# A hybrid diffusion backbone on one core: gate matrices without their zero halves, their products on quarters of the array

## The chip, the cores and the metric

The kernel runs on one core of one Trainium2 chip. The metric is the device time of one execution in microseconds (us). TensorE (PE) multiplies matrices into PSUM, which has eight banks here; VectorE (DVE), ScalarE (ACT) and GpSimd (POOL) compute; SyncE (SP) issues every DMA.

## The reference

Two layers work on 256 latent tokens with 256 context tokens ahead of them, 1024 channels, all in fp32. Each layer projects its modulated, normalised input to three mixers, merges them and ends with a mixture of experts. The change touches the first mixer, a gated linear recurrence that runs forwards and backwards (the direction index is di):

```python
def lru_scan(u, wa, ba, wx, bx, lam, h0, reverse):
    ub = u.reshape(B, L, LRU_HEADS, LRU_BW)             # 16 heads of 64 channels
    r = sigmoid(einsum('blhi,hij->blhj', ub, wa) + ba)
    i = sigmoid(einsum('blhi,hij->blhj', ub, wx) + bx)
    log_a = -LRU_C * r * softplus(-lam)
    a = exp(log_a)
    b = sqrt(-expm1(2.0 * log_a)) * (i * u)
    a_cum, b_cum = associative_scan(_linear_combine, (a, b), reverse=reverse, axis=1)
    return a_cum * h0[:, None, :] + b_cum
```

Every head multiplies its 64 channels by a 64x64 matrix, once for the r gate (wa) and once for the i gate (wx), for each direction.

## The kernel before

Activations lie transposed: 128 channels on the partitions, 512 tokens (context, then latent) along the free axis. `Dense` (from L152) runs the large projections. A step loads a block of 1024x256 weights (`raw`, two buffers), splits it on ACT (`whi`, L179 or L225) and DVE (`wlo`, L180 or L226) into a high and a low part, and multiplies: 48 matmuls of 512 columns into a pair of PSUM tiles `pT` (`Dense.T`, L207 to L209; `Dense.first`, L238 to L240, is the first two steps of layer 0 at once, half of the contraction at a time), or 96 of 256 columns into `pN` (`Dense.N`, L258 to L260). The weights of a step are split while the step before runs. After every 12 matmuls of a T step and 24 of an N step `tick` (L458) runs one piece of pending work from a list; the mixers' element work and their small products get between the large ones in this way. In layer 0 ticks also run a piece of `mod_vec`, the later modulation vectors (`psmod`, L412, fp32 products on column groups of 32).

`lru` (L588) makes the recurrence in four blocks of 256 channels. `lru_block` (L596) takes the projections `ax` and `ay` of its block, convolves `ax` to `u` (two tiles of 128 channels, kk = 0 and 1, two heads each), and leaves seven pieces of work for later ticks: four calls of `gates(kk, di)`, one square root, two scans. `gates` (L615) multiplies `u` by the r and the i matrix (`zr` L622, `zi` L623), each a PSUM tile of 512 columns, and hands on to ACT: `tr` (L625) from zr, `lT` (L627), `lQ` (L628), then `ti` (L631) from zi. A bank is free again when ACT has read it. The two heads of a tile are multiplied at once: `load_lru_w` (L575) lays their 64x64 matrices on the diagonal of a 128x128 one; POOL zeroes the tile (L578), and eight DMAs fill the diagonal (L584). One tile holds one block's matrices, and each block loads the next one's.

All PSUM tiles come from one pool of eight banks. At the start `norm1` (L517) transposes the normalised input into eight PSUM tiles `psu` (L539), which are all the banks; ACT and DVE copy them out (`u`, L546). Then `vectors` (L358) and `mod_half` (L433 to L451) use banks again: 64 small fp32 products `psmod` (L441) per half, a row `modrow`, a transpose `pst`, the copy `modT`; after that ACT and DVE modulate `u` (L561, L562) and split it to `uhi` and `ulo` (L488, L489), which the first dense step needs. The second half of `mod_half` follows in the middle of `Dense.first`.

The order of instructions on each engine is made by a scheduler when the program is built, from the data they need and from costs that it assumes; an instruction marked with `keep_in_program_order` keeps its place among the others so marked. An engine runs its instructions in that order.

Of the kernel before, what the change touches and what calls it, by code (L numbers as in the profile page):

```python
# [14 lines left out]
AF = mybir.ActivationFunctionType  # L15
# [3 lines left out]
P = 128  # L19
# [65 lines left out]
def body(ctx: ExitStack, tc: tile.TileContext, A, cst, at, out):  # L85
    nc = tc.nc
# [8 lines left out]
    def T(tag, shape, dt=F32, name=None):  # L95
        cnt[0] += 1
        n = int(np.prod(shape[1:]))
        if tag in BUFS:
            assert n <= SIZE[tag], (tag, shape)
            return sb.tile(list(shape), dt, tag=tag, bufs=BUFS[tag], name=f"{name or tag}_{cnt[0]}",  # L100
                           padded_shape=[P, *shape[1:]] if shape[0] != P else None)
        return sb.tile(list(shape), dt, tag=tag, name=f"{name or tag}_{cnt[0]}")
# [5 lines left out]
    def PS(shape, name="ps"):  # L108
        cnt[0] += 1
        return psp.tile(list(shape), F32, tag="ps", bufs=8, name=f"{name}_{cnt[0]}")  # L110

    act, dve, pool, pe = nc.scalar, nc.vector, nc.gpsimd, nc.tensor
# [230 lines left out]
    for n, tag in enumerate(["yhl"] * 4 + ["y32"] * 2 + ["mg"] * 2):  # L343
        half, i, kq = n // 4, 1 - n // 2 % 2, n % 2
# [228 lines left out]
    lru_w = {}  # L573

    def load_lru_w(L, c):  # L575

        wb = lru_w[L, c] = T("t4", [P, 2, 4, P], name="lruw")
        ms = pool.memset(wb, 0.0)  # L578
        if L and c == 0:
            tc.keep_in_program_order(ms)  # L580
        for di in range(2):
            for ty, nm in enumerate(("lru_wa", "lru_wx")):
                for par in range(2):
                    nc.sync.dma_start(  # L584
                        wb[64 * par:64 * par + 64, :, 2 * di + ty, 64 * par:64 * par + 64],
                        A[nm][L, di, 4 * c + par:4 * c + 4:2].rearrange("k i j -> i k j"))

    def lru(L, dn, u, q0, between):  # L588
        vt = vec[L]
        y = [T("y32", [P, 4, 512], name="ya") for _ in range(2)]  # L590
        for c in range(4):
            lru_block(L, dn, u, q0, vt, y, c)
            between(c)
        return y

    def lru_block(L, dn, x, q0, vt, y, c):  # L596
        wb = lru_w.pop((L, c))
        if c < 3:
            load_lru_w(L, c + 1)
        px, py = dn.first(x) if dn.at == 0 and q0 == 0 else (dn.T(x, 0, 512), None)  # L600
        us = []
        for kk in range(2):
            k = 2 * c + kk
# [8 lines left out]
            us.append(u.rearrange("p s n -> p (s n)"))  # L612
        st = {}

        def gates(kk, di):  # L615
            if not st:
                tags = ("yhl", "mg", "mg") if L and c % 2 else ("yhl",) * 3
                st.update((n, T(tag, [P, 4, 512], name="l" + n)) for n, tag in zip("TQG", tags))
            Tt, Q, G = st["T"], st["Q"], st["G"]
            k, i4, uf = 2 * c + kk, 2 * kk + di, us[kk]  # L620
            zr, zi = PS([P, 512], "zr"), PS([P, 512], "zi")
            pe.matmul(zr, wb[:, kk, 2 * di], uf, start=True, stop=True)  # L622
            pe.matmul(zi, wb[:, kk, 2 * di + 1], uf, start=True, stop=True)  # L623
            tr = T("t2", [P, 512], name="tr")
            act.activation(tr, zr, AF.Tanh, scale=0.5, bias=vt[:, 48 + 8 * di + k:49 + 8 * di + k])  # L625
            o = 16 * L + 8 * di + k
            act.activation(Tt[:, i4], tr, AF.Tanh, scale=spm[:, 0, o:o + 1], bias=spm[:, 0, o:o + 1])  # L627
            act.activation(Q[:, i4], tr, AF.Exp, scale=spm[:, 1, o:o + 1], bias=spm[:, 1, o:o + 1])  # L628
            dve.scalar_tensor_tensor(Q[:, i4], Q[:, i4], 1.0, Tt[:, i4], op0=ALU.add, op1=ALU.mult)
            ti = T("t2", [P, 512], name="ti")  # L630
            act.activation(ti, zi, AF.Tanh, scale=0.5, bias=vt[:, 64 + 8 * di + k:65 + 8 * di + k])  # L631
            dve.scalar_tensor_tensor(G[:, i4], ti, 1.0, uf, op0=ALU.add, op1=ALU.mult)

        py = py or dn.T(x, q0, 512)
# [34 lines left out]
        for kk in range(2):  # L669
            for di in range(2):  # L670
                pend.append(lambda kk=kk, di=di: gates(kk, di))
# [807 lines left out]
    for L in range(DEPTH):  # L1479
        q0 = 0 if L == 0 else SEG  # L1480
        dn = dns[L]
        if L == 0:
            load_lru_w(0, 0)
        u = norm1(L, hs)
        if L:
            dn.split(0)
            load_lru_w(1, 0)
        else:
            load_mask()
# [39 lines left out]
        r = norm2_router(L, vs, ss, q0, ex)  # L1529
# [41 lines left out]
```

## Time and profile before

| | |
|---|---|
| median of three runs | 2471.84 us (lowest 2471.45) |
| the profiled execution | 2469.8 us, its span 2468.0 us |
| PE busy | 2332.3 us, 95% of the span |
| DVE, ACT, POOL busy | 1273.3, 784.8, 69.9 us |
| mean granted clock of PE | 0.976 of full speed |
| DMA | 589.44 MB, mean 239 GB/s |

The first seven per cent of the span are the start and the recurrence of layer 0, from 71 to about 192 us; that of layer 1 lies between 1456 and 1587 us. Busy time is the union of an engine's instructions in a group or stretch. A matmul's duration counts from its start to its modelled end, so that consecutive matmuls overlap; the distance of their starts is what one costs.

### The profile page before, as it was taken

To read this page: it belongs to the slowest core of one execution; us is meant where nothing else is said; L and a number is where in the kernel's file an instruction comes from. 1 tells how busy PE (TensorE), PEld (TensorE's weight loads), DVE (VectorE), ACT (ScalarE), POOL (GpSimd) and SP (SyncE) were. 2 spreads that over 40 slices of the span, in tenths; PEclk is the share of its full clock that TensorE was granted. 3 is DMA by queue.
4 is the path that set the end of the run, shared out by engine and by line. 5 is a ranking of instruction groups with operands and counts; after the bars stand their busy time and mean duration, and the time that the engine had idled before them with its cause. 6 is when DMAs were issued, how large, how long until landed. Compare 5 with 4: busy or idle time off the path is not lost. (4 is left out here: it accounts for less than half of the span.)

```text
span 2468.0 us, 33524 instructions
## 1 busy us (share of the span) xinstructions
PE 2332.3 (95%) x13576; PEld 1586.1 (64%) x13576; DVE 1273.3 (52%) x2458; ACT 784.8 (32%) x1397; POOL 69.9 (3%) x99
## 2 busy tenths in 40 slices
PE   6999999999999989998999989999999889989997
PEld 5667787888888964445444367788889844333433
DVE  4796444367764552324233678776787632222224
ACT  3665222255543321000000166744555411010001
POOL 1000000000000000000000110000000000000001
PEclk8999999999999979999999989999999989999999
DMA  8655353221323557999899932233334889999997
GB/s 291 234 188 198 132 187 102 86 86 52 96 86 106 186 219 303 398 389 376 364 399 415 376 99 90 86 103 120 120 104 147 311 344 405 419 383 420 420 420 293
DMA packets 203709, 589.44 MB, mean 239 GB/s; under 512 B 24112, under 2 KB 135328, under 8 KB 154656
## 3 DMA queue, kind: packets, MB, share of 16 engines
q1 hardware_dynamic: 203552, 587.26, 62.6%
q8 instruction: 109, 1.79, 0.3%
q14 instruction: 48, 0.39, 0.1%
HBM read 585.05 MB, written 2.16 MB: 238 GB/s over the span
## 5 line engine op out<-in xcount | busy, mean ns | idle before, releaser
L180 DVE TENSOR_TENSOR wlo<-raw,whi 128x1024 fp32r<-128x1024 f32 x212 | 258.9, 1222 | 215.6 <-ACT whi L179 209.6
L179 ACT CAST whi<-raw 128x1024 fp32r<-128x1024 f32 x212 | 222.5, 1050 | 353.6 <-PE pT L208 283.3
L207 PE MATMUL pT<-uhi,whi 128*128 128x512 f32 (+1 forms) x896 | 331.0, 370 | 2.3 <-ACT uhi L488 2.3
L209 PE MATMUL pT<-uhi,wlo 128*128 128x512 f32 (+1 forms) x896 | 315.6, 352 | 0.0
L208 PE MATMUL pT<-ulo,whi 128*128 128x512 f32 (+1 forms) x896 | 315.0, 352 | 0.0
L1239 PE MATMUL pdn<-we,hT 128*64 128x512 f32 x1024 | 260.6, 607 | 35.9 <-DMA we<-in_expert_w_down_dram 35.9
L1239 PE MATMUL pup<-we,xT 128*64 128x512 f32 x1024 | 231.5, 593 | 1.5 <-DMA we<-in_expert_w_up_dram 1.5
L1239 PE MATMUL pgate<-we,xT 128*64 128x512 f32 x1024 | 231.0, 603 | 0.0
L1239 PEld LDWEIGHTS pdn<-we,hT 128*64 128x64 f32 x1024 | 83.7, 139 | 203.4 <-issue 129.5
L207 PEld LDWEIGHTS pT<-uhi,whi 128*128 128x128 f32 x896 | 169.7, 190 | 39.0 <-issue 12.6
L208 PEld LDWEIGHTS pT<-ulo,whi 128*128 128x128 f32 x896 | 169.8, 190 | 26.1 <-issue 4.9
L209 PEld LDWEIGHTS pT<-uhi,wlo 128*128 128x128 f32 x896 | 169.3, 189 | 25.1 <-issue 1.1
L1328 ACT CAST myh<-pdn 128x512 fp32r<-128x512 f32 x64 | 37.6, 587 | 457.2 <-PE pdn L1239 457.2
L1239 PEld LDWEIGHTS pup<-we,xT 128*64 128x64 f32 x1024 | 75.2, 137 | 150.7 <-issue 143.7
L1239 PEld LDWEIGHTS pgate<-we,xT 128*64 128x64 f32 x1024 | 71.3, 139 | 140.1 <-issue 137.2
L258 PE MATMUL pN<-whi,uhi 128*128 128x256 f32 x512 | 151.2, 295 | 0.0
L259 PE MATMUL pN<-wlo,uhi 128*128 128x256 f32 x512 | 145.6, 284 | 5.6 <-DVE wlo L180 5.5
L1329 DVE TENSOR_TENSOR myl<-pdn,myh 128x512 fp32r<-128x512 f32 x64 | 44.0, 688 | 198.1 <-ACT myh L1328 198.1
L260 PE MATMUL pN<-whi,ulo 128*128 128x256 f32 x512 | 145.4, 284 | 0.0
L207 PE MATMUL pT<-yhi,whi 128*128 128x512 f32 (+1 forms) x384 | 132.4, 345 | 0.0
L209 PE MATMUL pT<-yhi,wlo 128*128 128x512 f32 (+1 forms) x384 | 129.4, 337 | 0.0
L208 PE MATMUL pT<-ylo,whi 128*128 128x512 f32 (+1 forms) x384 | 129.4, 337 | 0.0
(335 smaller groups left out, 3995.6 us busy)
## 6 DMA issues: line engine op xcount, KB each, us to landing
we<-in_expert_w_down_dram SPq DMA_DIRECT2D x128, 1024.0 KB
we<-in_expert_w_gate_dram SPq DMA_DIRECT2D x127, 1024.0 KB
we<-in_expert_w_up_dram SPq DMA_DIRECT2D x125, 1024.0 KB
raw<-in_w_in_dram SPq DMA_DIRECT2D x76, 1024.0 KB
wmod<-in_w_mod_dram SPq DMA_DIRECT2D x48, 1024.0 KB
raw<-in_w_branch_a_dram SPq DMA_DIRECT2D x8, 1024.0 KB
raw<-in_w_branch_b_dram SPq DMA_DIRECT2D x8, 1024.0 KB
raw<-in_w_branch_c_dram SPq DMA_DIRECT2D x8, 1024.0 KB
```

The lines of the kernel that those rows point to most:

```text
L179: act.copy(hi, raw[:, 4 * kh:4 * kh + 4])
L180: dve.tensor_sub(lo, raw[:, 4 * kh:4 * kh + 4], hi.bitcast(F32))
L207: pe.matmul(ps[j], wh, xhi(kk)[:, n0:n1], start=kk == 0, stop=False)
L208: pe.matmul(ps[j], wh, xlo(kk)[:, n0:n1], start=False, stop=False)
L209: pe.matmul(ps[j], wl, xhi(kk)[:, n0:n1], start=False, stop=kk == 7)
L258: pe.matmul(ps[:, i], xh, wh, start=kk == 0, stop=False)
L259: pe.matmul(ps[:, i], xh, wl, start=False, stop=False)
L260: pe.matmul(ps[:, i], xl, wh, start=False, stop=kk == 7)
L1239: keep(pe.matmul(*a, **k))
L1328: act.copy(yh[:, cc], pd)
L1329: dve.tensor_sub(yl[:, cc], pd, yh[:, cc].bitcast(F32))
```

## The change

The gate matrices are stored as they come, without zeros: a tile `wb` of 4 heads' pairs by 4 matrices by 64 columns has the matrices of two blocks, so that two loads per layer remain of four, with eight DMAs each, and no memset. The products of both directions of a tile are issued together by a new function `products(kk)`, called by `gates(kk, 0)`: four PSUM tiles at once, and eight products of 64 rows by 64 columns, each on a quarter of the array. Head h of the tile takes rows 64h; its zr goes to columns 64h and its zi to columns 64(1 - h). The first four products are head 0 of di 0 and head 1 of di 1, the other four the rest; each four cover the four quarters of the array and write four different tiles. All are marked `keep_in_program_order`. The halves of zi come out swapped, so `ti` is made by two activations of 64 partitions, each reading the other half of zi.

```diff
     def load_lru_w(L, c):
-        wb = lru_w[L, c] = T("t4", [P, 2, 4, P], name="lruw")
-        ms = pool.memset(wb, 0.0)
-        if L and c == 0:
-            tc.keep_in_program_order(ms)
+        wb = T("t4", [P, 4, 4, 64], name="lruw")
+        for i in range(2):
+            lru_w[L, c + i] = wb[:, 2 * i:2 * i + 2]
         for di in range(2):
             for ty, nm in enumerate(("lru_wa", "lru_wx")):
                 for par in range(2):
-                    nc.sync.dma_start(
-                        wb[64 * par:64 * par + 64, :, 2 * di + ty, 64 * par:64 * par + 64],
-                        A[nm][L, di, 4 * c + par:4 * c + 4:2].rearrange("k i j -> i k j"))
+                    nc.sync.dma_start(wb[64 * par:64 * par + 64, :, 2 * di + ty],
+                                      A[nm][L, di, 4 * c + par:4 * c + 8:2].rearrange("k i j -> i k j"))
...
         wb = lru_w.pop((L, c))
-        if c < 3:
-            load_lru_w(L, c + 1)
+        if c == 1:
+            load_lru_w(L, 2)
...
+        zs = {}
+
+        def products(kk):
+            uf, quarters = us[kk], [[], []]
+            for di in range(2):
+                zs[kk, di] = PS([P, 512], "zr"), PS([P, 512], "zi")
+                for h in range(2):
+                    for ty in range(2):
+                        quarters[di ^ h].append((di, h, ty, 64 * (h ^ ty)))
+            for di, h, ty, o in quarters[0] + quarters[1]:
+                r = 64 * h
+                tc.keep_in_program_order(
+                    pe.matmul(zs[kk, di][ty][o:o + 64], wb[r:r + 64, kk, 2 * di + ty], uf[r:r + 64], start=True, stop=True,
+                              tile_position=(r, o)))
+
         def gates(kk, di):
...
-            zr, zi = PS([P, 512], "zr"), PS([P, 512], "zi")
-            pe.matmul(zr, wb[:, kk, 2 * di], uf, start=True, stop=True)
-            pe.matmul(zi, wb[:, kk, 2 * di + 1], uf, start=True, stop=True)
+            if di == 0:
+                products(kk)
+            zr, zi = zs.pop((kk, di))
...
             ti = T("t2", [P, 512], name="ti")
-            act.activation(ti, zi, AF.Tanh, scale=0.5, bias=vt[:, 64 + 8 * di + k:65 + 8 * di + k])
+            for r in (0, 64):
+                act.activation(ti[r:r + 64], zi[64 - r:128 - r], AF.Tanh, scale=0.5,
+                               bias=vt[r:r + 64, 64 + 8 * di + k:65 + 8 * di + k])
             dve.scalar_tensor_tensor(G[:, i4], ti, 1.0, uf, op0=ALU.add, op1=ALU.mult)
```

With the change the scheduler makes another order, also in places whose code is the same. Three of them follow.

ACT at the start, before: `xn` is the normalised input, `u` the copies out of the transposes' banks, `whi` the casts of weight blocks (raw_124 is the first block, raw_130 the second).

```order
L528 ACTIVATE xn_162<-h_5_86,rs_176 128x1024
L546 COPY u_231<-psu_192 128x512
L546 COPY u_234<-psu_194 128x512
L546 COPY u_237<-psu_196 128x512
L546 COPY u_240<-psu_198 128x512
L561 ACTIVATE u_231<-u_231,modT_58_326,a_50_249 128x256 x2
L488 CAST uhi_187<-u_231 128x512 x2
L561 ACTIVATE u_234<-u_234,modT_58_326,a_50_249 128x256 x2
L488 CAST uhi_187<-u_234 128x512 x2
L225 CAST whi_410<-raw_124 128x1024
```

The same place on ACT with the change:

```order
L528 ACTIVATE xn_161<-h_5_86,rs_175 128x1024
L225 CAST whi_399<-raw_124 128x1024
L225 CAST whi_403<-raw_130 128x1024
L225 CAST whi_548<-raw_124 128x1024
L546 COPY u_230<-psu_191 128x512
L546 COPY u_233<-psu_193 128x512
L546 COPY u_236<-psu_195 128x512
L546 COPY u_239<-psu_197 128x512
L561 ACTIVATE u_230<-u_230,modT_58_325,a_50_248 128x256 x2
L488 CAST uhi_186<-u_230 128x512 x2
```

Three casts, one of them of the second block, now stand ahead of the copies; on DVE the three subtractions that belong to them stand ahead of its four copies in the same way. On SP the DMAs of both blocks stand where they stood.

PE with the change, in layer 0, second call of `products` of the second block (`zr` and `zi` are the quarters, the `pT` around them a dense step):

```order
L627 MATMUL zr_1064<-lu_828,lruw_151 64x512
L627 MATMUL zi_1065<-lu_828,lruw_151 64x512
L207 MATMUL pT_982<-uhi_188,whi_839 128x512
...
L627 MATMUL zr_1066<-lu_828,lruw_151 64x512
...
L627 MATMUL zi_1067<-lu_828,lruw_151 64x512
L627 MATMUL zr_1064<-lu_828,lruw_151 64x512
L627 MATMUL zi_1065<-lu_828,lruw_151 64x512
L627 MATMUL zr_1066<-lu_828,lruw_151 64x512
L627 MATMUL zi_1067<-lu_828,lruw_151 64x512
```

Before, each call of `gates` has one zr and one zi of 128x512 here, 12 pT apart. Now the call is in three pieces: two, one and five quarters. The second calls of the third and the fourth block of layer 0 are in two pieces of two and six, with 12 pT between; the other thirteen calls stand in one piece of eight.

ACT in layer 1, second block, before: from the first gate's `lT` to the cast of the weights that the next dense step needs.

```order
L627 ACTIVATE lT_11698<-tr_11705,spm 128x512
L643 ACTIVATE gx_11654<-gx_11654 128x256
L628 ACTIVATE lQ_11699<-tr_11705,spm 128x512
L631 ACTIVATE ti_11710<-zi_11702,vec_347 128x512
L625 ACTIVATE tr_11741<-zr_11737,vec_347 128x512
L631 ACTIVATE ti_11746<-zi_11738,vec_347 128x512
L627 ACTIVATE lT_11698<-tr_11741,spm 128x512
L628 ACTIVATE lQ_11699<-tr_11741,spm 128x512
L625 ACTIVATE tr_11778<-zr_11774,vec_347 128x512
L631 ACTIVATE ti_11783<-zi_11775,vec_347 128x512
L627 ACTIVATE lT_11698<-tr_11778,spm 128x512
L179 CAST whi_11669<-raw_11586 128x1024
```

The same stretch with the change:

```order
L642 ACTIVATE lT_11724<-tr_11739,spm 128x512
L643 ACTIVATE lQ_11725<-tr_11739,spm 128x512
L647 ACTIVATE ti_11744<-zi_11728,vec_346 64x512 x2
L640 ACTIVATE tr_11772<-zr_11729,vec_346 128x512
L647 ACTIVATE ti_11777<-zi_11730,vec_346 64x512
L642 ACTIVATE lT_11724<-tr_11772,spm 128x512
L643 ACTIVATE lQ_11725<-tr_11772,spm 128x512
L647 ACTIVATE ti_11777<-zi_11730,vec_346 64x512
L640 ACTIVATE tr_11818<-zr_11806,vec_346 128x512
L647 ACTIVATE ti_11823<-zi_11807,vec_346 64x512
L642 ACTIVATE lT_11724<-tr_11818,spm 128x512
L179 CAST whi_11695<-raw_11612 128x1024
```

Ahead of the cast stand five half `ti` where three whole ones stood, and one `gx` has gone ahead of `lT`; the rest is the same.

## Rows read from the trace of the kernel before

**Rows 1.** The page's first line: span of the profiled execution.

```profile
span 2468.0 us, 33524 instructions
```

**Rows 2.** Stretches: us, busy (instructions) per engine, PEclk, DMA share, GB/s.

```profile
core 0: us, PE busy (x) PEld busy (x) DVE busy (x) ACT busy (x) POOL busy (x), PEclk, DMA share, GB/s
17.50:32.10 14.60, 5.88 (x132) 4.47 (x133) 8.15 (x26) 6.41 (x12) 0.95 (x1) 0.70 0.97 331
106.40:140.37 33.97, 33.97 (x177) 22.46 (x176) 30.11 (x47) 23.18 (x31) 0.31 (x1) 1.00 0.57 195
1497.03:1535.49 38.46, 35.99 (x210) 29.47 (x210) 30.40 (x49) 24.73 (x36) 0.00 (x0) 1.00 0.28 89
```

**Rows 3.** Groups by line: names, form, count | busy us, mean ns | idle.

```profile
L1239 PEld LDWEIGHTS pgate<-we,xT 128*64 128x64 f32 x1024 | 71.3, 139 | 140.1 <-issue 137.2 <-DVE acc L1356 2.1
...
L412 PE MATMUL psmod<-wmod,sT 128*32 128x256 f32 x640 | 43.7, 391 | 0.0
...
L622 PE MATMUL zr<-lu,lruw 128*128 128x512 f32 x64 | 32.9, 595 | 2.5 <-ACT rv L778 1.6 <-issue 0.9
...
L623 PE MATMUL zi<-lu,lruw 128*128 128x512 f32 x64 | 32.7, 592 | 0.0
...
L631 ACT ACTIVATE ti<-zi,vec 128x512 f32<-128x512 f32 x32 | 21.8, 680 | 0.7 <-PE zi L623 0.7
...
L895 ACT COPY yc<-pay 64x256 f32<-64x256 f32 x24 | 8.8, 367 | 15.4 <-DVE yc L897 15.0
```

**Rows 4.** Timeline of PE, gate products of layer 0, and expert products: start, duration.

```profile
72.05 1.02 PE L623 MATMUL zi<-lu,lruw 128*128 128x512 f32 x2
...
73.00 1.07 PE L412 MATMUL psmod<-wmod,sT 128*32 128x256 f32 x16
...
74.00 0.50 PE L207 MATMUL pT<-uhi,whi 128*128 128x512 f32 x1
...
74.33 0.39 PE L208 MATMUL pT<-ulo,whi 128*128 128x512 f32 x1
...
74.56 0.40 PE L209 MATMUL pT<-uhi,wlo 128*128 128x512 f32 x1
...
902.80 3.65 PE L1239 MATMUL pgate<-we,xT 128*64 128x512 f32 x16
```

**Rows 5.** Timeline of the start, all engines: start us, duration us.

```profile
16.64 2.49 DVE L546 COPY u<-psu 128x512 f32<-128x512 f32 x4 [2.93 <-PE psu L539]
...
16.75 2.06 ACT L546 COPY u<-psu 128x512 f32<-128x512 f32 x4 [3.72 <-PE psu L539]
...
17.62 2.83 PE L441 MATMUL psmod<-wmod,sT 128*32 128x128 f32 x96
...
23.76 1.94 PE L441 MATMUL psmod<-wmod,sT 128*32 128x128 f32 x32 [3.06 <-DMA wmod<-in_w_mod_dram]
...
32.10 0.79 PE L238 MATMUL pT<-uhi,whi 128*128 128x512 f32 x1 [5.11 <-ACT whi L225]
...
35.79 1.99 ACT L225 CAST whi<-raw 128x1024 fp32r<-128x1024 f32 x2 [1.17 <-DMA raw<-in_w_in_dram]
...
39.60 2.35 DVE L226 TENSOR_TENSOR wlo<-raw,whi 128x1024 fp32r<-128x1024 f32 x2
...
48.63 3.48 PE L441 MATMUL psmod<-wmod,sT 128*32 128x128 f32 x118
...
54.74 1.20 PE L238 MATMUL pT<-uhi,whi 128*128 128x512 f32 x4 [1.90 <-ACT uhi L488]
...
65.77 0.40 PE L240 MATMUL pT<-uhi,wlo 128*128 128x512 f32 x1
```

**Rows 6.** Timeline of layer 1, second block: ACT and then PE.

```profile
1498.16 0.69 ACT L625 ACTIVATE tr<-zr,vec 128x512 f32<-128x512 f32 x1 [3.84 <-PE zr L622]
...
1506.72 1.05 ACT L179 CAST whi<-raw 128x1024 fp32r<-128x1024 f32 x1
...
1497.03 1.10 PE L622 MATMUL zr<-lu,lruw 128*128 128x512 f32 x2 [0.86 <-issue]
...
1509.38 0.79 PE L207 MATMUL pT<-uhi,whi 128*128 128x512 f32 x1
```

## The prediction

> **What bounds the kernel now.** I read the page first (its span is 2468.0 us [rows 1]), then the stretches in which the gate products run, then the groups by line, and then the timelines at three places. The reader is to see three things.
>
> First, the stretches: in a block of layer 0 TensorE (PE) is busy for all 33.97 us and VectorE (DVE) for 30.11; in a block of layer 1 PE has 35.99 of 38.46 us, DVE 30.40, ScalarE (ACT) 24.73 [rows 2]. PE sets the pace, DVE is close behind, and what PE saves there counts only until DVE or ACT is late.
>
> Second, the gate products. 64 zr and 64 zi instructions are 32 calls of each, every fp32 product being two passes [rows 3]. Two passes last 1.02 us and one 0.592, so passes start 0.43 us apart [rows 3, 4]. 128 passes are 55 us of PE, half of it multiplying stored zeros.
>
> Third, the start. PE's matmuls of the first dense step begin at 32.10; the modulation products of the first half (17.62 and 23.76) come right after ACT and DVE have copied the eight transposed tiles out of PSUM (16.75 and 16.64, each x4) [rows 5]. Those tiles fill all eight PSUM banks, so nothing of PE's goes on before some are copied out. The second weight block, raw 1, lands at 35.79: there ACT's cast ends a wait on it [rows 5].
>
> **The change, part by part.**
>
> *Passes.* 16 calls of products issue 8 quarters of 2 passes: 256 passes. Run four at a time they are 64 waves of 0.43 = 27.5 us, and PE saves 27.5. The trace has no quarter of the rows. It has column tiles: 640 psmod passes over four column groups make 43.7 us busy, 0.07 each where one lasts 0.39, and 16 of them fit in 1.07 us; 16 pgate passes on two column groups take 3.65 us, (3.65 - 0.59) / 7 = 0.44 per pair [rows 3, 4]. Four weights and four moving operands on the same rows do run together. The unknown is two row groups at once. Bounds: four at a time as psmod (27.5 saved), one at a time as zr (256 x 0.43 = 110, so 55 lost). I take four, the nearest row being psmod, and because the four quarters of a wave go to four banks.
>
> *Switching.* Between full-array and tiled work PE loses time: the second zi pass ends streaming at 72.05 + 0.86 = 72.91 and psmod starts at 73.00; psmod's last wave is over near 73.9 and pT starts at 74.00 [rows 4]. That is 0.1 us a side. The scheduled order has the 16 calls in 20 bursts, so 40 x 0.1 = 4 us. Three calls of layer 0 are split, because their second pair of banks comes later: with two or three pieces they need 6, 6 and 8 waves in place of 4, another 8 x 0.43 = 3.4. PE's own saving is 27.5 - 4 - 3.4 = 20.
>
> A page of the Trainium skill speaks against this. Of packed tiles it says (TensorE: Matmul & The Clock Gate, Part 3, "What overlaps and what doesn't") that a weight load hides under running matmuls only where the row group differs. Here zr and zi of one half share a row group. Taken at its word each wave would add a load of 0.139 us [rows 3], 64 x 0.139 = 9 us, and the saving would be 11. The pgate row has the same rows in every pass and 0.44 us a pair, so nothing is added there, and I leave it out of the sum.
>
> *ACT.* ti is read in two halves of 64 partitions. Row for row that is 32 more instructions. Bounds: half of 0.68 each (no extra work) or 0.68 each (32 x 0.68 = 22 us more). The 64-partition copy of 256 columns takes 0.367, over half of what 512 columns on 128 partitions take, so partitions don't count and I take 0.68 [rows 3]. ACT has room on average (24.73 of 38.46 [rows 2]), but not in the burst. In layer 1's second block the gate chain begins at 1498.16 and the next weight cast, behind it in ACT's queue, at 1506.72; PE needs that block at 1509.38 [rows 6]. Now: zr is complete only when both groups of waves are, so the chain starts 0.85 later, near 1499.0; the order puts five half ti before the cast in place of three whole ones, 2 x 0.57 = 1.1 more (0.57 from start to start). The cast then starts near 1508.1 and ends at 1509.1. PE, with two bursts of 1.9 in place of four gates of 1.71, is there 3.0 us earlier, at 1506.4, and waits 2.7: three blocks give 0.3 to 0.7 each, 1.5 in all. The first block has its gates between longer steps; I take 2. In layer 0 the first block's 3.0 are taken whole; in the other three one call is split (1.5 + 0.45 or less of 3.4), four banks are held until ACT has read the late half of ti, and DVE has 30.11 us of work in a block that could shrink to 32 [rows 2]; I take 1 together. Gates: 1.5 + 2 + 3.0 + 1 = 7.5 us gained. The bounds are 20 (ACT and DVE never late) and 0 (all given back).
>
> *Start.* The scheduler has moved three casts of weights on ACT, and their subtractions on DVE, ahead of the copies out of PSUM. The second needs raw 1, and that DMA stands where it stood behind the same megabytes. So: the casts end at 35.79 + 1.99 = 37.8; DVE subtracts twice behind the cast of raw 1 (from 36.8, 2.35 for two) until 39.2, and its first copy is out near 39.9 (2.49 for four) [rows 5]. The psmod bank is the one DVE frees. 128 psmod passes: 96 took 2.83 and, after idling, 32 took 1.94 [rows 5]; the granted clock of that stretch is 0.70 on average, so between 1.2 and 2.4 GHz [rows 2]. PE will have idled for 20 us, so the low level is likely: 4 to 7 us, I take 6.5, to 46.4. From the end of such products to the first matmul took 54.74 - (48.63 + 3.48) = 2.6 [rows 5]: 49.0 in place of 32.10. The 48 matmuls of the first half at 0.23 [rows 4] take 11.1, plus 1 for operands that are late: 61. The second half follows as before after 54.74 - 48.63 = 6.1 and takes 65.77 + 0.23 - 54.74 = 11.3 [rows 5]: 78.5 in place of 66.0. That is 12.5 us late; as PE is full in the blocks behind it [rows 2], nothing takes it up. I take 13, between 9 and 17 (psmod at either clock, and up to 4 us for operands or a low clock in the first half).
>
> *Nothing.* The eight POOL memsets go, and half of the gate weights' DMAs, whose issues stand on SP behind raw 1 and behind all that the first step needs. The first load carries 0.26 MB more; at the 331 GB/s of the start [rows 2] that is 0.8 us for what follows it, covered by the late start itself.
>
> *Sum.* -7.5 + 13 = +5.5. The profiled execution took 2469.8, so 2475.3; the median of the runs is 2.0 above it, so 2477.
>
> **The rivals.**
>
> A, the gain arrives whole: ACT's and DVE's order adapt without waits. For it: both are idle for part of every block [rows 2]. Against: the cast's place in ACT's queue. 2471.8 - 20 + 13 = 2465.
>
> B, the start is hardly late: the copies wait, but what follows closes up to 3 us. For it: PE was waiting there anyway (5.11 before 32.10 [rows 5]), and afterwards all weights of the first half lie ready. Against: the transposes' banks hold up every product behind them. 2471.8 - 7.5 + 3 = 2467.
>
> C, two at a time: row groups take turns. Then 128 waves are 55 us, as before, and the switches are lost: 2471.8 + 4 + 13 = 2489.
>
> D, one at a time: the quarters do not run together at all. 256 x 0.43 = 110, so 2471.8 + 55 + 4 + 13 = 2544, slower by 2.9%. It decides from the point at which the gates lose 36 us, that is when fewer than about 1.3 passes run at once. For it: no pass on a row group beside another is in the trace. Against: the column tiles.
>
> E, evacuation is the bound: every saved microsecond of PE is waited for at ACT's reads of the gates. Gates 0, 2471.8 + 13 = 2485. Beside it stands the Trainium skill, TensorEngine Tiling (Array Packing), "PSUM Bottleneck": tiling speeds up TensorE but not the emptying of PSUM, and the copy may become the bottleneck. What the trace shows of it is the cast 2.7 us before PE's need in layer 1.
>
> **How the numbers follow.** My forecast 0.52, A 0.14, B 0.06, C 0.12, D 0.08, E 0.08. A measurement of this kernel tells about 2%, 49 us, from no change; only D is outside: slower 0.08, within 0.90, faster 0.02 (nothing in the sum reaches it). The bounds of the two terms together, -20 + 9 and 0 + 17, give 2461 and 2489; C at the start's upper bound is 2493. The range is 2460 to 2496 and holds all but D and the tails of the others.
>
> **What would show it.** Right: zr and zi passes starting in fours some ns apart, each wave 0.43 behind the last; ACT idle from about 13 until raw 1 lands, and the first pT near 49; in layer 1 waits of PE on ACT's cast right behind the gates. Wrong: the first pT near 32; quarter passes 0.43 apart one by one; no PE wait in the blocks, and blocks of layer 1 a full 3 us shorter.

## The result, and the profile after

The changed kernel takes 2505.07 us (median of 4 runs, 2502.13 to 2508.04), the kernel before 2471.64 beside it: a ratio of 1.0143, 95% interval 1.0122 to 1.0164. That is within the 2% about which the chances were given, but the whole interval lies above 1, and the time is outside the predicted range of 2460 to 2496. The ratio leaves out one slow run of the kernel before (3831.83 us) and, like those below, is not quite the quotient of the two medians.

The page and the groups by line of the changed kernel, which answer to [rows 1, 3] (`zr`, `zi` at L627 and `ti` at L647 are L622, L623, L631 of before):

```profile
span 2504.7 us, 33747 instructions
...
PE 2325.4 (93%) x13704; PEld 1577.0 (63%) x13704; DVE 1272.5 (51%) x2458; ACT 809.4 (32%) x1429; POOL 61.4 (2%) x91
```

```profile
L647 ACT ACTIVATE ti<-zi,vec 64x512 f32<-64x512 f32 x64 | 43.7, 683 | 2.5 <-PE zi L627 1.0
L627 PE MATMUL zr<-lu,lruw 64*64 64x512 f32 x128 | 37.9, 646 | 12.1 <-ACT ti L647 11.3 <-ACT rv L795 0.7
L627 PE MATMUL zi<-lu,lruw 64*64 64x512 f32 x128 | 37.9, 647 | 0.0
```

A half ti of 64 partitions costs 683 ns where a whole one cost 680: ACT has 24.6 us more work. And zr now has 11.3 us of waiting for that ti, where before it had none.

PE at the first call of products, answering to [rows 4]:

```profile
85.25 0.64 PE L627 MATMUL zr<-lu,lruw 64*64 64x512 f32 x1
85.26 0.64 PE L627 MATMUL zi<-lu,lruw 64*64 64x512 f32 x1
...
85.73 0.59 PE L627 MATMUL zr<-lu,lruw 64*64 64x512 f32 x1
...
86.16 0.59 PE L627 MATMUL zr<-lu,lruw 64*64 64x512 f32 x1
...
87.13 1.07 PE L412 MATMUL psmod<-wmod,sT 128*32 128x256 f32 x16
```

Four quarter passes start within 0.02 us, the next four 0.43 to 0.48 later: a whole call lasts 1.88 us. Four quarters work at a time, as the change has it.

The start, answering to [rows 5]:

```profile
26.55 1.04 ACT L225 CAST whi<-raw 128x1024 fp32r<-128x1024 f32 x1 [14.05 <-DMA raw<-in_w_in_dram]
...
34.98 1.99 ACT L225 CAST whi<-raw 128x1024 fp32r<-128x1024 f32 x2 [7.39 <-DMA raw<-in_w_in_dram]
...
36.88 2.04 ACT L546 COPY u<-psu 128x512 f32<-128x512 f32 x4
...
39.08 5.60 PE L441 MATMUL psmod<-wmod,sT 128*32 128x128 f32 x128 [1.14 <-DVE u L546]
...
47.45 1.20 PE L238 MATMUL pT<-uhi,whi 128*128 128x512 f32 x4 [1.59 <-ACT uhi L488]
```

ACT waits for two weight blocks, 14.05 and 7.39 us, before it copies anything out of PSUM; the first dense matmul is at 47.45 in place of 32.10.

Where the time went can be read by laying the two traces side by side, one execution of each kernel: the start of the same instruction in both, at the first zr (71.19 before), in the retention, the mixer behind layer 0's recurrence (pN, 270.09), at layer 1's first transpose (psu, 1423.87), in its retention (prs, 1640.01) and at the last matmul (2456.35). The table gives what is lost between one mark and the next, in us, for this kernel and for the runs of the next section:

| | until first zr | layer 0's recurrence | attention, experts | layer 1's recurrence | rest |
|---|---|---|---|---|---|
| predicted | +13 | -4.0 | 0 | -3.5 | 0 |
| the changed kernel | +14.1 | +12.4 | +0.8 | +9.3 | +0.1 |
| e1 copies first | +22.8 | +11.4 | -5.1 | +8.1 | +2.8 |
| e2 per direction | +21.9 | +9.3 | -0.1 | +7.2 | +4.6 |
| e3 one ti | +22.5 | +3.8 | +46.2 | -4.7 | +2.9 |
| e4 before, split ti | +0.3 | +9.3 | +1.9 | +10.0 | -0.1 |
| e5 memset back | -2.8 | +11.9 | -6.2 | +11.2 | +3.0 |
| e6 swapped u | -2.8 | +2.0 | +0.6 | -4.0 | +0.1 |
| e7 two at a time | -2.0 | +4.2 | -3.4 | +2.6 | +0.1 |
| e8 swapped u, four banks | -3.3 | +6.1 | +0.5 | -0.3 | -0.2 |

The column of attention and experts, whose code is the same everywhere, moves by some us either way from kernel to kernel; only the start and the two recurrences are read.

**Layer 0.** The second call of products in the second block, on ACT and then on PE, and the granted clock of the stretches around it:

```profile
127.67 1.03 ACT L179 CAST whi<-raw 128x1024 fp32r<-128x1024 f32 x1
128.60 0.81 ACT L642 ACTIVATE lT<-tr,spm 128x512 f32<-128x512 f32 x1
...
130.15 1.38 ACT L647 ACTIVATE ti<-zi,vec 64x512 f32<-64x512 f32 x2
...
131.57 1.81 PE L627 MATMUL zr<-lu,lruw 64*64 64x512 f32 x2 [4.35 <-ACT ti L647]
...
133.91 0.63 PE L209 MATMUL pT<-uhi,wlo 128*128 128x512 f32 x1
...
173.46 1.07 PE L627 MATMUL zr<-lu,lruw 64*64 64x512 f32 x2 [1.75 <-ACT ti L647]
...
212.52 1.11 PE L627 MATMUL zr<-lu,lruw 64*64 64x512 f32 x1 [5.24 <-ACT ti L647]
```

```profile
core 0: us, PE busy (x) PEld busy (x) DVE busy (x) ACT busy (x) POOL busy (x), PEclk, DMA share, GB/s
116.38:158.99 42.61, 38.26 (x194) 22.40 (x193) 32.17 (x49) 27.09 (x35) 0.31 (x1) 0.88 0.45 150
...
131.57:142.50 10.93, 10.93 (x25) 4.97 (x26) 3.78 (x6) 7.95 (x12) 0.00 (x0) 0.53 0.27 92
...
173.46:176.03 2.57, 2.57 (x13) 0.79 (x13) 1.01 (x2) 2.54 (x4) 0.00 (x0) 1.00 1.05 361
...
212.52:216.00 3.48, 3.48 (x12) 1.30 (x12) 1.68 (x3) 3.43 (x5) 0.00 (x0) 0.50 0.83 282
216.00:223.00 7.00, 7.00 (x22) 4.92 (x20) 2.49 (x5) 6.65 (x11) 0.00 (x0) 0.68 0.00 0
...
1521.09:1562.94 41.85, 34.44 (x224) 28.89 (x225) 30.66 (x49) 28.02 (x39) 0.00 (x0) 0.92 0.23 76
...
1555.66:1558.00 2.34, 2.34 (x11) 2.34 (x12) 2.34 (x4) 0.58 (x3) 0.00 (x0) 0.50 0.00 0
```

PE stands 4.35 us for a bank that ACT frees with the second half of ti, and then works 10.93 us at a granted clock of 0.53, which is nearly all at the 1.2 GHz level: by an estimate from that clock another 5 us. The block takes 42.61 us where one took 33.97 [rows 2]. The same wait comes twice more, 1.75 us at 173.46 and 5.24 at 212.52; behind the short one the clock stays at 1.00, behind the long one it is 0.50 again.

**Layer 1.** A block takes 41.85 us where it took 38.46 [rows 2]. Its chain after, from ACT to DVE to PE (`lT` L665 is the square root, `lT` L672 the first scan operation; the block's first zr is at 1521.09):

```profile
1523.07 0.69 ACT L640 ACTIVATE tr<-zr,vec 128x512 f32<-128x512 f32 x1 [0.73 <-PE zi L627]
...
1541.95 1.92 ACT L665 ACTIVATE lT<-lT 128x2048 f32<-128x2048 f32 x1
...
1543.78 2.92 ACT L179 CAST whi<-raw 128x1024 fp32r<-128x1024 f32 x3
...
1543.90 1.29 DVE L672 SCALAR_TENSOR_TENSOR lT<-lQ,lT 128x512 f32<-128x512 f32 x2 [2.00 <-ACT lT L665]
...
1554.39 1.21 DVE L180 TENSOR_TENSOR wlo<-raw,whi 128x1024 fp32r<-128x1024 f32 x1
...
1555.66 0.58 PE L259 MATMUL pN<-wlo,uhi 128*128 128x256 f32 x1 [6.28 <-DVE wlo L180]
```

The same chain in the kernel before (first zr at 1497.03 [rows 6]):

```profile
1514.54 1.92 ACT L648 ACTIVATE lT<-lT 128x2048 f32<-128x2048 f32 x1
...
1526.97 1.23 DVE L180 TENSOR_TENSOR wlo<-raw,whi 128x1024 fp32r<-128x1024 f32 x1
...
1528.25 0.39 PE L259 MATMUL pN<-wlo,uhi 128*128 128x256 f32 x1 [1.35 <-DVE wlo L180]
```

The square root comes 20.86 us behind the first zr in place of 17.51, 3.35 later: 0.85 of it pass until the first `tr`, and from there ACT works with only 0.4 us of idle time and takes 18.88 us where it took 16.38. From the square root's start to the subtraction of wlo it is 12.44 and 12.43 us. So wlo is 3.4 us later, PE is there earlier, and waits 6.28 in place of 1.35. The block is longer by 3.39, just what ACT is late. Behind this wait the clock is down too, at 0.50 until 1558.00, but from the matmul that waited to the next block's first zr it is 7.28 us, where it was 7.24: here the low clock costs nothing.

### The profile page after: what moved, and what is told of

It is laid out like the page before. It is cut to its first block, busy times and chain, and to the rows that moved or that the text cites. A ratio compares the mean times of both kernels' runs of the same rounds, so it can differ in the third digit from the quotient of the medians.

```text
span 2504.7 us, 33747 instructions
## 1 busy us (share of the span) xinstructions
PE 2325.4 (93%) x13704; PEld 1577.0 (63%) x13704; DVE 1272.5 (51%) x2458; ACT 809.4 (32%) x1429; POOL 61.4 (2%) x91
## 5 line engine op out<-in xcount | busy, mean ns | idle before, releaser
L207 PE MATMUL pT<-uhi,whi 128*128 128x512 f32 (+1 forms) x896 | 325.3, 364 | 1.6 <-ACT uhi L488 1.6
```

Source lines behind the costliest of these rows:

```text
L207: pe.matmul(ps[j], wh, xhi(kk)[:, n0:n1], start=kk == 0, stop=False)
```

## The experiments

**e1, copies first.**

```diff
-                (act.copy if k % 2 else dve.tensor_copy)(us[k], pss[k])
+                tc.keep_in_program_order((act.copy if k % 2 else dve.tensor_copy)(us[k], pss[k]))
...
-                    act.copy(hi, self.raws[c][:, 4 * kh:4 * kh + 4])
-                    dve.tensor_sub(lo, self.raws[c][:, 4 * kh:4 * kh + 4], hi.bitcast(F32))
+                    tc.keep_in_program_order(act.copy(hi, self.raws[c][:, 4 * kh:4 * kh + 4]))
+                    tc.keep_in_program_order(dve.tensor_sub(lo, self.raws[c][:, 4 * kh:4 * kh + 4], hi.bitcast(F32)))
```

> The changed kernel, but the four copies out of PSUM on ACT and the four on DVE keep their place ahead of the weight casts and subtractions of the first dense step, as before. Theory (the start is late by what the first gate burst shows, 85.25 against 71.19, and nothing later takes that up): first pT near 32 and the first burst near 71, time 2505.1 - 14 = 2491. Rival (the late start only hides a wait that the blocks of layer 0 would have anyway): first pT near 32, but the waits of TensorE in layer 0 grow by as much, time 2500 to 2506.

2512.17 us (ratio 1.0187, 1.0169 to 1.0205). The first pT is back at 32.88, but the first zr comes at 93.99, later yet. DVE and then PE of this run:

```profile
50.56 0.29 DVE L129 CAST amr<-am 128x256 fp32r<-128x256 f32 x1 [13.60 <-DMA am<-in_const_dram]
50.76 2.36 DVE L226 TENSOR_TENSOR wlo<-raw,whi 128x1024 fp32r<-128x1024 f32 x2
...
52.04 0.80 PE L240 MATMUL pT<-uhi,wlo 128*128 128x512 f32 x1 [15.42 <-DVE wlo L226]
```

The marks moved something else: a cast of the attention mask stands ahead of wlo on DVE and waits 13.60 us for its own DMA. So this run tells nothing of either theory's start; e5 does.

**e2, per direction.** As e1, and `products(kk, di)` issues the four quarters of one direction into its two banks, called by every `gates`:

```diff
-            for di, h, ty, o in quarters[0] + quarters[1]:
...
+            for h in range(2):
+                for ty in range(2):
+                    r, o = 64 * h, 64 * (h ^ ty)
...
```

> As the run with the mended start, but the products are issued per direction again: one call writes two PSUM tiles with four quarters (four quarters of the array at once, two to a bank) and not four tiles with eight. Theory for layer 0 (TensorE waits 4.5, 1.9 and 5.4 us in the second call of three blocks because a call needs four banks and ACT has two of them still to read): these waits go and the clock that falls behind them too, 10 to 16 us less than the run with the mended start, near 2478; layer 1 gains 0 to 3. Rival (what counts is ACT's longer work, whoever holds the banks): the waits move to other instructions, time within 3 us of the run with the mended start. Second rival (two quarters to one bank do not run together): passes of a call 0.43 apart in pairs or singly, 14 us or more on top.

2514.23 us (1.0183, 1.0158 to 1.0208), within 3 us of e1, as the first rival has it. The recurrences are 9.3 and 7.2 late against 11.4 and 8.1 of e1. Two quarters to one bank do run together (the four zr and zi of a call start within 0.02 us).

**e3, one ti.** As e1, with

```diff
-            for r in (0, 64):
-                act.activation(ti[r:r + 64], zi[64 - r:128 - r], AF.Tanh, scale=0.5,
-                               bias=vt[r:r + 64, 64 + 8 * di + k:65 + 8 * di + k])
+            act.activation(ti, zi, AF.Tanh, scale=0.5, bias=vt[:, 64 + 8 * di + k:65 + 8 * di + k])
```

> As the run with the mended start, but ti is one activation of 128 partitions, which leaves the two heads of the i gate exchanged (the kernel leaves the swap out, nothing else). Theory for layer 1 (four more half ti of 0.57 in each block put the last weight casts on ACT 2.3 us of 3.4 later, so the raw buffer comes free late, the next block of weights lands late and TensorE waits 5 to 6.4 us for wlo): the waits for wlo shrink to those of before, 2 us a block, and the time falls by 9 to 14 us, in layer 0 by another 2 to 4: near 2478. Rival (the chain is late because zr is complete only after both waves, 0.85 us, or because of the four banks): less than 4 us of fall.

2536.19 us (1.0273, 1.0256 to 1.029), but 46 us of that lie in the experts: this kernel computes other gate values, so tokens go to other experts, and a loop that takes tokens beyond an expert's places runs in this trace alone (152 matmuls, `xpgate` among them, from 1180.6 to 1226.6). Read by the table, layer 0 is 3.8 late in place of 11.4, and layer 1 is 4.7 early in place of 8.1 late. What the theory says of ti holds in both layers, by 20 us together, in layer 0 with more than it gave. Its path through the raw buffer does not (e9), and the three later waits for wlo of layer 1 only fall from 6.3 to between 3.3 and 4.1.

**e4, the kernel before with ti split.** Whole products, the start of before:

```diff
-            act.activation(ti, zi, AF.Tanh, scale=0.5, bias=vt[:, 64 + 8 * di + k:65 + 8 * di + k])
+            for r in (0, 64):
+                act.activation(ti[r:r + 64], zi[r:r + 64], AF.Tanh, scale=0.5,
+                               bias=vt[r:r + 64, 64 + 8 * di + k:65 + 8 * di + k])
```

> The kernel before, with whole 128x128 products, but ti made by two activations of 64 partitions each (nothing exchanged): the price of ACT's 32 more instructions alone, with no change of the weights, the products or the start. Theory (ACT's chain sets when the weights of layer 1 come): the casts of a layer 1 block come 2.3 us later, waits for wlo grow by 1 to 2.3 us in three blocks and less in layer 0, time 2475 to 2480. Rival (ACT has room, only the four banks and the start count): 2470 to 2473.

2488.10 us against 2467.97 (1.0078, 1.0061 to 1.0095): 20 us, far more than either side said. The waits of its PE in layer 0 and in layer 1 (us in total, times, longest):

```profile
PE zr L622 <- ACT ti L632: 6.4, 2, 4.4
...
PE pN L259 <- DVE wlo L180: 13.6, 5, 4.7
```

32 more activations, 22 us of ACT's time, are nearly all paid at the end of the program, on an engine that is busy a third of the span. In layer 0 PE waits for a bank that ti holds although each call takes only two.

**e5, the memset back.**

```diff
         wb = T("t4", [P, 4, 4, 64], name="lruw")
+        ms = pool.memset(wb, 0.0)
+        if L and c == 0:
+            tc.keep_in_program_order(ms)
```

> The changed kernel with the POOL memset of the gate weights put back (it zeroes a tile that the DMAs then fill whole, so it is of no use): with it the scheduler makes the order of before at the start, copies out of PSUM first. Theory (the start costs what the first gate burst shows, 14 us, and the rest is ACT's split ti, which alone cost the kernel before 20 us): first burst near 71, time 2505 - 14 = 2491, 2487 to 2495. Rival (as the run with the mended start seemed to say, the blocks of layer 0 wait anyway): first burst near 71 and 2500 or more.

2490.97 us (1.01, 1.0081 to 1.0118), as the theory has it: 14.1 less than the changed kernel, or 10.6 by the two ratios. ACT copies out of PSUM first again, with no wait for a weight block:

```profile
16.45 2.05 ACT L546 COPY u<-psu 128x512 f32<-128x512 f32 x4 [3.67 <-PE psu L539]
```

The first zr comes 2.8 us earlier than in the kernel before (e6 to e8 have this too, e4 does not; its cause is not shown), the recurrences stay 11.9 and 11.2 late. So it was the missing memset, an instruction of an engine that is nearly idle, that made the scheduler put casts that wait for DMAs ahead of the copies.

**e6, swapped u.** As e5; POOL exchanges the halves of u, the i gate's rows in the weights lie the other way round, and `products(kk, di)` issues per direction into two banks, as in e2:

```diff
-                    nc.sync.dma_start(wb[64 * par:64 * par + 64, :, 2 * di + ty],
+                    nc.sync.dma_start(wb[64 * (par ^ ty):64 * (par ^ ty) + 64, :, 2 * di + ty],
...
+        sw = T("t4", [P, 2, 512], name="lus")
+        for kk in range(2):
+            for r in (0, 64):
+                pool.tensor_copy(sw[r:r + 64, kk], us[kk][64 - r:128 - r])
...
+            for h in range(2):
+                for ty, uf in enumerate((us[kk], sw[:, kk])):
+                    r, o = 64 * (h ^ ty), 64 * h
...
+            act.activation(ti, zi, AF.Tanh, scale=0.5, bias=vt[:, 64 + 8 * di + k:65 + 8 * di + k])
```

> As the run with the memset back, but the swap is taken out of ACT: POOL makes a copy of u with its two halves of partitions exchanged (four copies of 64x512 a block), the i gate's matrices lie on the other half of the rows, so that zi comes out straight and ti is one activation again; products per direction, four quarters at a time into two banks. Theory (ACT's 32 more activations are the loss, the quarters themselves a gain): layer 0 gains 4 to 12 us against before, layer 1 0 to 4, time 2455 to 2466. Rival (what TensorE saves is waited for at ACT's and DVE's weight splits, whatever ti costs): 2467 to 2474. Second rival (POOL's copies hold up the products or DVE): waits of TensorE on lus, 2475 or more.

2462.12 us against 2468.45, a ratio of 0.9976 (0.9964 to 0.9987): the fastest of all, a little faster than both kernels, and inside what was expected. It came otherwise, though: layer 1 gains 4.0, layer 0 gains nothing behind the first zr (+2.0), and the start is 2.8 earlier. In layer 0 PE still waits 3.48 us once for a bank that ti holds, and the clock is 0.50 for the 5.64 us behind it, from 153.67 on; e7 has neither. POOL's copies (median 0.61 us) hardly hold PE up: its waits for `lus` are 0.3 us together.

**e7, two at a time.** As e6 without the copies: zr and zi of a head both on the head's own columns.

```diff
+            for ty in range(2):
+                for h in range(2):
+                    r = 64 * h
+                    tc.keep_in_program_order(
+                        pe.matmul(zs[kk, di][ty][r:r + 64], wb[r:r + 64, kk, 2 * di + ty], uf[r:r + 64], start=True, stop=True,
+                                  tile_position=(r, r)))
```

> As the run with swapped u, without the copies: zr and zi of a head both go to the head's own columns, so nothing is swapped, ti is one activation, and only two of the four quarters of the array work at a time (128 waves of 0.43 in place of 64). It has the small weights, the memset and 64x64 products, and TensorE's time of before. Theory: time of before and 2 to 4 us of switches, 2469 to 2473. The difference to the run with swapped u is what the second pair of quarters is worth; rival (64x64 products cost something by themselves, as weight loads on the same rows that are not hidden): 2476 or more.

2470.36 us (1.0015, 1.0003 to 1.0027), as the theory has it. Small products two at a time cost 2 us in all (by the table 6.8 in the recurrences, which the start and the other parts give back in part), and the other two quarters of the array are worth 8 (2470.36 - 2462.12) once ACT's work is the same.

**e8, swapped u and four banks.** e6 with the eight quarters of both directions issued together again:

```diff
-            products(kk, di)
+            if di == 0:
+                products(kk)
```

> As the run with swapped u (2462), but the products of both directions are issued together again, eight quarters into four banks as in the changed kernel: the price of holding four banks, without ACT's longer work. Theory (four banks at once cost waits of TensorE in the second call of three blocks of layer 0, and the gate chain starts 0.85 us later in each block): layer 0 5 to 10 us worse than with two banks, layer 1 1 to 3 worse, 2467 to 2474. Rival (as the two runs with split ti said, 2512 and 2514: four or two banks is the same): 2459 to 2465.

2473.34 us (1.0016, 0.9996 to 1.0035; 2466.27 to 2480.69), as the theory has it: about 10 more than e6, layer 0 and layer 1 each some 4 us worse. Here the four banks do cost; between e1 and e2, with ti split, the same two columns differ by 3 together. Why it is less there is not shown.

**e9, three raw buffers.** As e5.

```diff
-    BUFS = {"uT": 4, "yhl": 4, "y32": 2, "mg": 2, "raw": 2, "ws": 6, "dc": 1, "t4": 7, "t2": 11, "da": 1}
+    BUFS = {"uT": 4, "yhl": 4, "y32": 2, "mg": 2, "raw": 3, "ws": 6, "dc": 1, "t4": 6, "t2": 9, "da": 1}
```

> As the run with the memset back (2491), but with three raw buffers in place of two; the room comes from one t4 buffer less and two t2 buffers less. Theory (in layer 1 TensorE waits 6.45 us three times because the late third cast frees a raw buffer late, and the DMA into it takes 6.4 us): these waits fall to 2 or less, layer 1 from +12 to 0 to +4 against before, 2478 to 2484, unless the missing t2 buffers give waits elsewhere, in layer 0 too. Rival (the cast itself is late by its place behind the gates on ACT, whenever the data come): the waits stay over 4 us, 2488 to 2494.

2490.99 us (1.0085, 1.0055 to 1.0114): the theory of the raw buffer falls, the wait in layer 1 stays as it was. DVE and PE:

```profile
1523.08 1.29 DVE L675 SCALAR_TENSOR_TENSOR lT<-lQ,lT 128x512 f32<-128x512 f32 x2 [2.00 <-ACT lT L668]
...
1533.56 1.22 DVE L180 TENSOR_TENSOR wlo<-raw,whi 128x1024 fp32r<-128x1024 f32 x1
...
1534.84 0.58 PE L259 MATMUL pN<-wlo,uhi 128*128 128x256 f32 x1 [6.28 <-DVE wlo L180]
```

The subtraction is again 10.48 us behind the first scan operation, though the data lie there: DVE's order decides. The trace of the changed kernel said so already. ACT and DVE go through the weight blocks in the same order, so the cast that belongs to the subtraction of 1554.39 is the second of the three at 1543.78, over by 1545.75, 8.6 us before it, as in this run. The block that lands last before that subtraction, at 1552.75, is the next one, and the 0.6 us with which e11 and e13 reckon below are a misreading.

**e10, e11, e12, the subtraction kept in place.** In layer 1 the subtractions of the weight splits and the first operation of each scan piece are marked; e10 on e9, e11 on e5, e12 on e6.

```diff
-                    dve.tensor_sub(lo, raw[:, 4 * kh:4 * kh + 4], hi.bitcast(F32))
+                    sub = dve.tensor_sub(lo, raw[:, 4 * kh:4 * kh + 4], hi.bitcast(F32))
+                    if self is dns[1] and self.at < 14:
+                        tc.keep_in_program_order(sub)
...
-                dve.scalar_tensor_tensor(Tt[:, i4], Q[:, i4], 2.0, Tt[:, i4], op0=ALU.add, op1=ALU.mult)
+                first = dve.scalar_tensor_tensor(Tt[:, i4], Q[:, i4], 2.0, Tt[:, i4], op0=ALU.add, op1=ALU.mult)
+                if L:
+                    tc.keep_in_program_order(first)
```

> As the run with three raw buffers (2491), but in layer 1 DVE's subtractions of the weight splits keep their place of the program, ahead of the first operation of each scan piece that comes later in the program. Theory (TensorE waits for a wlo that stands on DVE behind ten operations of the scans, 10.5 us after the square root on ACT in every kernel; what split ti moves is that square root; the data and the cast are there 4 us earlier with three raw buffers): the three waits of 6.45 fall to 1 to 3, layer 1 from +10.7 to +1 to +4 against before, 2480 to 2485. Rival (cast or data are late as well): waits over 5, 2488 to 2494.

> The same order on DVE with two raw buffers (the run with the memset back, 2491, plus the order). Theory (the raw buffer comes free behind the same square root and its DMA lands only 0.6 us before DVE's place in the run of the changed kernel, so both chains have to be shortened): the waits stay at 5 to 6.5, 2486 to 2492. Rival (DVE's place alone decides): as the run with three raw buffers and the order.

> The run with swapped u (2462) with the same order on DVE: in layer 1 it has three waits for wlo of 2.5, 2.5 and 3.9 us. Theory: they fall to about 1 each unless the data are late (two raw buffers), 2456 to 2461. Rival (data late, or the scans pushed back hold up the gated products of the recurrence): 2461 to 2466.

2517.48, 2524.52 and 2506.65 us (1.0208, 1.0243, 1.0159): against every expectation, since the scans come earlier in the program than I took them to, and the marks put the subtraction behind all of them. Yet it shows the mechanism from the other side. In e10 it stands 18.2 us behind the first scan operation in place of 10.5, and PE's wait is 14.63 in place of 6.28:

```profile
1537.12 0.68 DVE L677 SCALAR_TENSOR_TENSOR lT<-lQ,lT 128x512 f32<-128x512 f32 x1
...
1555.34 1.21 DVE L180 TENSOR_TENSOR wlo<-raw,whi 128x1024 fp32r<-128x1024 f32 x1
...
1556.60 0.58 PE L261 MATMUL pN<-wlo,uhi 128*128 128x256 f32 x1 [14.63 <-DVE wlo L180]
```

**e13 to e16, the scans later.** Three empty entries in layer 1's list ahead of the scans; e13 on e5, e14 on e9, e15 on e6, e16 on e6 with the buffers of e9.

```diff
         for kk in range(2):
+            if L and not kk:
+                pend.extend([lambda: None] * 3)
             pend.append(lambda kk=kk: scan(kk))
```

> The run with the memset back (2491), with three empty entries in layer 1's list of pending work ahead of the two scan pieces, so that the scans come three ticks later; the order then has the critical subtraction three or four scan operations behind the square root on DVE, not ten. Two raw buffers. Theory with two chains (DVE's place, and the raw buffer that comes free behind the same square root with its data 0.6 us ahead): the three waits of 6.45 stay at 5 to 6.2, 2486 to 2492. Rival (DVE's place alone): waits 1 to 3, 2479 to 2484.

> The same with three raw buffers (one t4 and two t2 buffers less). Theory (both chains shortened): the waits fall to 1 to 3, layer 1 from +10.7 to 0 to +4, 2479 to 2485. Rival (the cast, or ACT's long gate chain itself, holds TensorE wherever DVE stands): waits over 4.5, 2487 to 2494.

> The run with swapped u (2462, waits of 2.5, 2.5 and 3.9 in layer 1) with the scans three ticks later, two raw buffers. Theory: the waits fall by 0 to 1 us each, the data being late then, 2459 to 2463; rival (the scans pushed back meet the next block's gates and cost): 2463 to 2468.

> The same with three raw buffers. Theory: the waits of layer 1 fall to about 0.5 to 1.5 each and TensorE's saving of 3 us a block arrives, 2453 to 2460; rival (missing t2 and t4 buffers cost in layer 0 what layer 1 gains): 2460 to 2466.

2492.37 (1.0103, 1.0073 to 1.0133), 2496.12 (1.0118, 1.0087 to 1.0149), 2468.43 (1.0, 0.9986 to 1.0015) and 2470.51 us (1.0013, 0.9999 to 1.0027): all four above everything expected of them, e13 and e15 by 0.4 us only, and none faster than the run it was made from. e13, DVE and PE:

```profile
1526.60 1.29 DVE L675 SCALAR_TENSOR_TENSOR lT<-lQ,lT 128x512 f32<-128x512 f32 x2 [2.00 <-ACT lT L668]
...
1532.88 1.21 DVE L180 TENSOR_TENSOR wlo<-raw,whi 128x1024 fp32r<-128x1024 f32 x1
...
1534.15 0.39 PE L259 MATMUL pN<-wlo,uhi 128*128 128x256 f32 x1 [1.05 <-DVE wlo L180]
```

With the subtraction 6.3 us behind the first scan operation the wait is 1.05, with two raw buffers: this wait is made by the subtraction's place on DVE, not by the data. But the time does not fall. Layer 1 is 14.9 us late in e13 where it was 11.2 in e5, in other waits:

```profile
PE pT L209 <- DVE wlo L180: 7.7, 3, 6.2
PE pT L207 <- ACT whi L179: 5.1, 3, 1.8
PE zi L630 <- ACT ti L650: 3.1, 1, 3.1
```

An order can move the wait, but it gave no time back: PE then waits elsewhere, for wlo, whi and ti. Only taking the work off ACT (e3, e6) made layer 1 shorter than before. Which of the new waits of e13 and e14 would be the next to mend stays open.

## Why the prediction was wrong

*Passes, switches: right.* 64 waves of 0.43, four at a time; a call lasts 1.88 us against four waves and a switch, 1.82. Rivals C and D are out. The Trainium skill (TensorE: Matmul & The Clock Gate, Part 3, "What overlaps and what doesn't") lets a weight load hide under running matmuls only where the row group differs. This trace does not agree: zr and zi of a head share their rows, and no wave has 0.139 us more, so the load was rightly left out of the sum. Of the 27.5 us of passes that four at a time save PE, the end of the program sees 8, and that only where ACT has no more to do (e6 against e7).

*Start: right, 14.1 at the first zr for 13.* It is the scheduler's doing and not the array's; with the order of before it is gone (e5). Rival B is out. The first pT was put at 49.0 and came at 47.45.

*ACT: the failed step.* The prediction took 0.68 for a half ti, 22 us more work, and then hid it: it gave ACT room on average (24.73 of 38.46) if not in the burst, named the cast of 1506.72 [rows 6] as the place where it shows, with a wait of PE of 2.7 us, and kept gains of 0.3 to 0.7 a block. The price was right, the cover was not there. At that cast PE does not wait: behind the gates of the changed block its first wait, of 1.02 us, ends at 1546.38. In layer 1 the deciding item was the square root at the end of the gate chain: it waits for all four gates, so it has all four more half ti (2.5 us with all that stands between) and the later zr (0.85) ahead of it, and scans, wlo and PE follow it at a fixed distance. The experiments bear that out. The second block of layer 1 takes 38.46 us before, 41.85 changed, 41.43 in e4, 37.60 in e3 and 38.20 in e6; from its square root to the next block's first zr it is 20.95, 20.99, 21.09, 20.98 and 20.99 us in the same order. Nearly all of the difference lies ahead of the square root. From the first `tr` to there ACT is idle for 0.79 us before and for less in the others, so there was no room in the burst. PE's waits of about 1 us for zr and wlo in the trace of before already said that a block of layer 1 is such a ring, in which PE's 35.99 of 38.46 us is not the bound. I read "PE sets the pace" from its busy share. Layer 1 was put at -3.5 and came at +9.3.

*Layer 0: the same, with a second term.* I took 1 us together for the three blocks with a split call, naming that four banks are held until ACT has read the late half of ti, and gave that no price. The three waits are 11.3 us, and the low clock behind the two long ones is worth another 9 by an estimate (10.93 us at 0.53; 3.48 at 0.50 and 7.00 at 0.68 behind 212.52). Layer 0 was put at -4 and came at +12.4. More of it is the split ti than the banks: 7.6 go with one ti (e3 against e1), 2.1 with two banks (e2 against e1).

*Rivals.* A is out with the gates' gain. E (2485, at 0.08) named the right engine, and had its price wrong by assuming that the loss ends at zero gain. An engine that gets more work in a ring can cost beyond what PE saved: e4 has the whole 20 us with no saving at stake. The Trainium skill (TensorEngine Tiling (Array Packing), "PSUM Bottleneck") says that tiling speeds up TensorE and not the emptying of PSUM. This trace goes further: emptying took longer, since the packing itself swapped the halves and doubled the number of reads of zi, at 683 ns each. The bounds of the gate term, 20 and 0 gained, were therefore no bounds: they should have gone below nothing, by the 22 us that stood in the same paragraph.

## What to carry to other kernels

Where engines hand work round in a ring (PE to ACT to DVE and back to PE), work added to one of them can count in full, as ACT's 22 us did here (e4), though its busy share over the span is a third; look for the last item of the chain, not the next one in the queue. If packing an array leaves its results in another place, let an idle engine move the input rather than a busy one the output. After an edit compare the order of every engine at the start, even for an instruction that was of no use: a scheduler may answer by putting a wait for a DMA ahead of what PE needs.

## What was not expected of the hardware

- An activation of 64 partitions by 512 takes 683 ns, one of 128 partitions 680.
- In layer 0, where PE is full, a wait of PE can cost more than its length: behind 4.35 us the granted clock was 0.53 for 10.93 us, behind 5.24 us 0.50 and then 0.68 for 10.5. Length alone does not tell: behind 1.75 us it stayed at 1.00, but in e3 it was 0.50 from 177.10 to 183.90, behind a wait of 1.53 that ended at 175.41.
- Four products of 64x64 on four quarters of the array start within 0.02 us of each other, into four banks or, two by two, into two (e2), at 0.41 to 0.48 us for a pass of 512 columns.
